# Layer 0's keys and values split straight into their attention tiles, with two tiles each, and the transposed maxima moved into the maxima's PSUM banks

## The chip, the cores and the metric

The kernel runs on one core of one Trainium2 chip. The time is the device time of one execution, in microseconds (us). The core has five engines that each work through a list of instructions of their own, strictly in order: TensorE (PE, matmuls; PEld is its weight load), VectorE (DVE), ScalarE (ACT), GpSimd (POOL) and SyncE (SP), which issues most DMA transfers. Engines wait for each other through semaphores.

## The reference

A two-layer model over 1024 latent tokens and 256 context tokens, width 1024. The change lies in layer 0, the even layer:

```python
aq, ak, av, ag, bq, bk, bv, bg = split_cols(h @ w_in, EVEN_WIDTHS)   # for latents and context
aq = rms_norm(heads(aq, A_HEADS), q_gain); ak = rms_norm(heads(ak, A_KV_HEADS), k_gain)
aq, ak, bq, bk = (apply_rope(t, cos, sin) for t in (aq, ak, bq, bk))  # latents only
oa = softmax(q k^T / 8) v     # branch A: every query block against all 1280 keys
ob = softmax(q k^T / 8 + band, sink) v   # branch B: context, and latents within +-128, with a sink logit
y = concat([oa * silu(ag), ob * silu(bg)]) @ w_out
```

Each branch has 8 query heads in 2 groups of 4 that share a key and value head. Layer 1 is a convolution module and a neighbourhood attention; its attention uses the same generator as layer 0's.

## The kernel before

All arithmetic is float32. A product is made from three matmuls of halves: each operand is split into a rounded high part (ACT copies it, L296) and the rest (`split`, L294 to 299, POOL or DVE subtracts). Layer 0 is cut into four **units**, one per key and value head: u = 2 and 3 are branch B, u = 0 and 1 branch A, in the order 2, 3, 0, 1 (`ORDER`).

- `proj_qkv(u)` (L772) projects 128 tokens at a time, ten blocks in five pairs, into PSUM (`pq`), copies them out (`pc`), norms and rotates them. `qk_tail` (L819) transposes a block (`trk`, in the one PSUM bank `tr`), splits queries and keys together (`qs`, 128x384) and stores them to DRAM (Q, K). Values are split into `vs` and stored to DRAM (V). `proj_gate` (L750, `pg`) makes the gates.
- Attention of a unit is ten groups of 128 queries x 4 heads (`group0`, L544). `attn_prep` (L378), two groups ahead, loads the queries (QH, QL), finds the maxima of the scores (`mx`, two PSUM banks, DVE reduces), and transposes them (`trn`, L404, in bank `tr`) into rows of QL. Then comes one **item** per 128 keys (L454): two matmuls to `st` (L463 against tile KA, L467 against tile KB), exp (L475), split into `ph` and `pl`, and `look` (3) items later three matmuls with the values (L426 to 428, `ov`). u = 2 and 3 have 42 items each, u = 0 and 1 have 84: 252 in all.
- KA (two buffers) holds the keys' high parts over their low parts; KB (one buffer) the high parts again and four rows of ones; V (one buffer) low and high values and a block of ones. All three are loaded from DRAM: KA in the prep of the unit's first group (`load_ka`, L535), KB at its first item (L540), V at its first `ov` (L629). The reload of KB and V must wait until the unit before has read them last. Earlier, the same SBUF holds modulation weights (`mw_tile`, L152).
- `weave` (L496) lays attention and **fill** side by side in the program: during a unit's attention the projections of the next one (`pq`, `pg`), during the last unit the output projection (`po`, L891). Fill has a lower priority, and a scheduler with a timeline of its own sets the final order on every engine, so a tile that it holds to be late draws fill forward.
- For the output projection `load_x1` (L883) loads the residual stream, 12 transfers on ACT's queue, between ACT's other work.

Of the kernel before, what the change touches and what calls it, by code (L numbers as in the profile page):

```python
# [87 lines left out]
def tile_kernel(ctx: ExitStack, tc: tile.TileContext, a, out):  # L88
# [22 lines left out]
    def nm(s):  # L111
        uid[0] += 1
        return f"{s}_{uid[0]}"
# [38 lines left out]
    def mw_tile():  # L152

        ring = MWR if mwp[0] is not None else "ABAV"
        mk[0] += 1
        t = ring[mk[0] % len(ring)]
        if t == "x":
            w = mwp[0].tile([P, 1024], F32, tag="mwx", name=nm("mw"), bufs=ring.count("x"))
        else:
            w = a0.tile([P, 1920 if t == "V" else NTOK], F32, tag={"A": "KA", "B": "KB", "V": "V"}[t], name=nm("mw"),  # L160
                        bufs=2 if t == "A" else 1)
        return w[:, 0:1024].rearrange("p (d n) -> p d n", d=2)
# [43 lines left out]
    def mod_steps(pool, halves):  # L206
# [10 lines left out]
        for n_, hf in enumerate(halves):  # L217
            for _ in range(4):
                yield
            tag = "ov" if solo[0] else "tr"  # L220
            pb = bank(tag, nm("pm"))
            for d, w in enumerate(ws):
                mod_part(pb, w, range(4 * d, 4 * d + 4))
            row = pool.tile([P, 512], F32, tag="macc", name=nm("mrow"), bufs=1)
            SC.copy(row, pb)
            yield
            yield
            mod_out(bank("ov" if solo[0] else "tr", nm("trm")), row, *hf)
# [149 lines left out]
    def attn_prep(pool, g):  # L378
# [22 lines left out]
        for _ in range(3):  # L401
            yield
        tr2 = bank("tr", nm("trn"))
        PE.transpose(tr2[0:nr, 0:P], nmt[:, 0:nr].bitcast(F32), ident)  # L404
# [111 lines left out]
    Qd = [[dram(f"Q{u}_{j}", [P, 2, 2, P]) for j in range(10)] for u in range(4)]  # L516
    Kd = [dram(f"K{u}", [64, 2, NTOK]) for u in range(4)]
    Vd = [dram(f"V{u}", [P, 10, P]) for u in range(4)]
    Gs = [dram(f"G{u}", [P, 2, NTOK]) for u in range(4)]
# [12 lines left out]

    KAs, KBs = [None] * 4, [None] * 4

    def load_ka(u):  # L535
        KAs[u] = a0.tile([P, NTOK], F32R, tag="KA", name=nm("KAt"), bufs=2)
        SY.dma_start(KAs[u][0:64, :].bitcast(F32), Kd[u][:, 0, :])
        SY.dma_start(KAs[u][64:128, :].bitcast(F32), Kd[u][:, 1, :])

    def load_kb(u):  # L540
        KB = KBs[0]
        SY.dma_start(KB[0:64, :].bitcast(F32), Kd[u][:, 0, :])

    def group0(u, qb):  # L544
        isb = u >= 2

        first = qb == QORD[0]

        def load_q(QH, QL):
            if first:  # L550
                load_ka(u)
            src = Qd[u][qb].rearrange("(e d) s a t -> d s e (a t)", e=2)
# [60 lines left out]
        def finish(ov, rb):  # L613
# [9 lines left out]
            else:  # L623
# [3 lines left out]

        hs = (u - 2) * 4
        g = Group(load_q=load_q, start=(lambda: load_kb(u)) if first else (lambda: None), bias=False, ahead=lambda t: None, gate=gate, v=lambda k: Vs[0][:, k, :], load_v=(lambda: SY.dma_start(Vs[0][:, :, 0:128].bitcast(F32), Vd[u])) if first else None, maxes=maxes, nmp=1 if qb < 2 else (2 if isb else 3),  # L629
                  sink=(sink[:, hs : hs + 4], sink8[:, hs : hs + 4]) if isb else None, skm=lambda: sk, k=lambda: (KAs[u], KBs[0]),  # L630
                  tiles=[(k, 0, 512, x) for k, x in kt], den=den, finish=finish)
# [6 lines left out]
    with ExitStack() as p0x:  # L638
# [133 lines left out]
        def proj_qkv(u, w):  # L772
            wh, wl = w or load_w0("ev_qkv", u)
            for jp in range(5):
                pc = ap.tile([P, 2, 384], F32, tag="pc", name=nm("pc"), bufs=PCB)
# [14 lines left out]
                if u < 2:  # L790
# [11 lines left out]
                SC.copy(vs[:, :, 1], pc[:, :, 320:384])  # L802
# [16 lines left out]
        def qk_tail(u, j, pc):  # L819

            tr = bank("tr", nm("trk"))
            for i in range(3):
                PE.transpose(tr[:, i * P : (i + 1) * P], pc[:, i * P : (i + 1) * P], ident)
# [726 lines left out]
```

## Time and profile before

| | |
|---|---|
| median of 3 runs | 1603.6 us (1599.02 to 1604.57) |
| the profiled execution, its own time | 1603.57 us |
| its span, first to last instruction | 1601.8 us |
| PE / DVE / POOL / ACT busy in the span | 92% / 67% / 49% / 46% |
| mean granted TensorE clock | 0.960 |
| bytes moved by DMA | 221.88 MB |

Layer 0's projections begin at 31 us, its attention at 149 us; its last item is at about 931 us. An engine's busy time is what its instructions took; since PE is near its limit, what counts is the time in which PE stood idle, and what it then waited for.

### The profile page before, as it was taken

To read this page: it belongs to the slowest core of one execution; us is meant where nothing else is said; L and a number is where in the kernel's file an instruction comes from. 1 tells how busy PE (TensorE), PEld (TensorE's weight loads), DVE (VectorE), ACT (ScalarE), POOL (GpSimd) and SP (SyncE) were. 2 spreads that over 40 slices of the span, in tenths; PEclk is the share of its full clock that TensorE was granted. 3 is DMA by queue.
4 is the path that set the end of the run, shared out by engine and by line. 5 is a ranking of instruction groups with operands and counts; after the bars stand their busy time and mean duration, and the time that the engine had idled before them with its cause. 6 is when DMAs were issued, how large, how long until landed. Compare 5 with 4: busy or idle time off the path is not lost.

```text
span 1601.8 us, 21782 instructions
## 1 busy us (share of the span) xinstructions
PE 1479.0 (92%) x7084; PEld 1181.1 (74%) x7084; DVE 1076.6 (67%) x2243; ACT 740.0 (46%) x1378; POOL 787.8 (49%) x632
## 2 busy tenths in 40 slices
PE   6899999998999989889999979999998899899995
PEld 2785978876788667668877757888877777777784
DVE  2921777497858677556488867999565476667776
ACT  4621343534344745644454754433343454545563
POOL 3530353554445755755554755654432343254575
PEclk9799999998999999989999989999999999999996
DMA  9476135342432123562111122213546777788732
GB/s 367 146 256 214 54 97 171 114 132 72 129 117 64 54 61 103 162 189 79 40 47 56 38 94 66 79 53 105 193 159 196 230 222 225 230 262 243 212 104 105
DMA packets 179194, 221.88 MB, mean 139 GB/s; under 512 B 16444, under 2 KB 120584, under 8 KB 179080
## 3 DMA queue, kind: packets, MB, share of 16 engines
q1 hardware_dynamic: 172416, 208.91, 42.2%
q10 hardware_dynamic: 6664, 11.57, 2.4%
q8 instruction: 56, 0.92, 0.2%
q14 instruction: 58, 0.48, 0.1%
HBM read 160.39 MB, written 60.03 MB: 138 GB/s over the span
## 4 chain that ended last, share of the span: by engine, by line
PE 66%; DVE 14%; DMA 8%; issue 6%; POOL 3%; ACT 2%; SPq 1%; DVEq 0%; ACTq 0%; POOLq 0%
PE p L317 5%; PE p L316 5%; PE p L318 5%; PE ov L426 4%; PE po L316 4%; PE ov L428 4%; PE ov L427 4%; PE po L317 4%; PE po L318 4%; PE st L463 3%; PE st L467 3%; PE pq L318 2%; PE pq L317 2%; PE pq L316 2%; PE pg L316 2%
## 5 line engine op out<-in xcount | busy, mean ns | idle before, releaser
L299 POOL TENSOR_TENSOR pl<-pf,ph 128x512 fp32r<-128x512 f32 (+4 forms) x321 | 391.7, 1233 | 341.2 <-ACT ph L296 294.8
L475 ACT ACTIVATE pf<-st 128x512 f32<-128x512 f32 x284 | 166.0, 597 | 212.7 <-PE st L467 158.4
L299 POOL TENSOR_TENSOR wl<-wr,wh 128x512 fp32r<-128x512 f32 (+2 forms) x131 | 169.4, 1306 | 172.0 <-ACT wh L296 146.5
L296 ACT CAST ph<-pf 128x512 fp32r<-128x512 f32 (+4 forms) x364 | 209.2, 588 | 32.3 <-PE ov L427 23.9
L316 PE MATMUL p<-hh,wh 128*128 128x512 f32 x448 | 181.3, 405 | 5.3 <-ACT hh L296 2.8
L317 PE MATMUL p<-hl,wh 128*128 128x512 f32 x448 | 180.0, 402 | 0.9 <-POOL hl L299 0.9
L318 PE MATMUL p<-hh,wl 128*128 128x512 f32 x448 | 177.7, 402 | 0.0
L463 PE MATMUL st<-QH,KAt 128*128 128x512 f32 (+4 forms) x364 | 142.9, 394 | 8.0 <-ACT pf L475 5.4
L426 PE MATMUL ov<-ph,Vt 128*128 128x512 f32 (+4 forms) x364 | 142.0, 390 | 5.8 <-DVE y L617 4.7
L428 PE MATMUL ov<-pl,Vt 128*128 128x512 f32 (+4 forms) x364 | 141.2, 388 | 3.9 <-DVE pl L299 2.5
L427 PE MATMUL ov<-ph,Vt 128*64 128x512 f32 (+4 forms) x364 | 139.8, 384 | 0.0
L467 PE MATMUL st<-QL,KBt 68*128 68x512 f32 (+4 forms) x364 | 137.7, 388 | 0.8 <-issue 0.8
L1035 DVE SCALAR_TENSOR_TENSOR cps<-U,taps,cps 128x512 f32<-128x512 f32 x184 | 126.3, 749 | 0.9
L296 ACT CAST wh<-wr 128x512 fp32r<-128x512 f32 (+2 forms) x134 | 80.7, 612 | 90.0 <-PE p L317 17.4
L580 DVE TENSOR_REDUCE mp<-mx 128x1 f32<-128x512 f32 x128 | 86.3, 683 | 53.4 <-PE mx L579 52.7
L316 PEld LDWEIGHTS p<-hh,wh 128*128 128x128 f32 x448 | 86.3, 193 | 27.3 <-ACT hh L296 3.0
L317 PEld LDWEIGHTS p<-hl,wh 128*128 128x128 f32 x448 | 85.9, 192 | 22.1 <-POOL hl L299 1.9
L318 PEld LDWEIGHTS p<-hh,wl 128*128 128x128 f32 x448 | 85.8, 191 | 20.0
L318 PE MATMUL pq<-wh,hl 128*128 128x384 f32 x256 | 89.4, 350 | 2.9 <-DVE hl L310 2.9
L316 PE MATMUL pq<-wh,hh 128*128 128x384 f32 x256 | 90.2, 352 | 0.8 <-ACT hh L296 0.7
L317 PE MATMUL pq<-wl,hh 128*128 128x384 f32 x256 | 89.3, 349 | 0.0
L428 PEld LDWEIGHTS ov<-pl,Vt 128*128 128x128 f32 x364 | 70.2, 193 | 25.8 <-POOL pl L299 3.8
(271 smaller groups left out, 3448.1 us busy)
## 6 DMA issues: line engine op xcount, KB each, us to landing
mw<-in_mod_w_dram SPq DMA_DIRECT2D x16, 1024.0 KB, 5.7
Q<-qs SPq DMA_DIRECT2D x40, 256.0 KB, 2.5
QH<-Q SPq DMA_DIRECT2D x80, 128.0 KB, 2.8
mw<-in_mod_w_dram SPq DMA_DIRECT2D x16, 512.0 KB, 7.2
wr<-in_od_d_dram SPq DMA_DIRECT2D x32, 256.0 KB, 2.8
wr<-in_ev_qkv_dram SPq DMA_DIRECT2D x16, 384.0 KB, 5.1
KAt<-KD SPq DMA_DIRECT2D x16, 384.0 KB, 6.5
wr<-in_od_wo_dram SPq DMA_DIRECT2D x22, 256.0 KB, 3.9
```

What stands on the lines that cost most here:

```text
L296: SC.copy(hi, src)
L299: (GP if leng == "g" else VE).tensor_tensor(lo, src, hi.bitcast(F32), op=ALU.subtract)
L316: PE.matmul(o, lh, rh, start=first, stop=False)
L317: PE.matmul(o, lh, rl, start=False, stop=False)
L318: PE.matmul(o, ll, rh, start=False, stop=last)
L426: PE.matmul(o, V[:, 64:192], ph[:, :n], start=(t == 0), stop=False)
L427: PE.matmul(g.ov[0:64, q0 : q0 + n], V[:, 0:64], ph[:, :n], start=False, stop=False)
L428: PE.matmul(o, V[:, 64:192], pl[:, :n], start=False, stop=(last and g.sink is None))
L463: sts.append(PE.matmul(st[:, :n], KA[:, cs], g.QH[:, q0 : q0 + n], start=True, stop=False))
L467: PE.matmul(st[:, :n], KB[0:68, cs], g.QL[0:68, q0 : q0 + n], start=False, stop=True)
L475: SC.activation(pf[:, :n], st[:, :n], AF.Exp, scale=1.0 if g.bias else SCALE)
L1035: VE.scalar_tensor_tensor(pc, uc, w, pc, op0=ALU.mult, op1=ALU.add)
```

## The change

Keys and values of layer 0 no longer pass through DRAM. `kv_tiles` allocates one KB, two KA and two V at the first projection (instead of at the start of the attention), and the units take turns on them. `qk_tail` splits the 64x128 of keys by two instructions of their own into KA, and the 128x256 of queries as before; `proj_qkv` writes the values' parts into V. KB is now loaded from KA, SBUF to SBUF, in two transfers (columns 0 to 511, then the rest), still at the unit's first item and still into one buffer. The transposed maxima (`trn`) take a bank of the maxima (`mx`) instead of `tr`, in both layers. Modulation weights may use two V buffers, and the row of a modulation product takes its memory from tag `rt2`.

```diff
@@ mw_tile
-                        bufs=2 if t == "A" else 1)
+                        bufs=1 if t == "B" else 2)
@@ mod_steps
-            row = pool.tile([P, 512], F32, tag="macc", name=nm("mrow"), bufs=1)
+            row = pool.tile([P, 640], F32, tag="rt2", name=nm("mrow"), bufs=2)[:, :512]
@@ attn_prep
-        tr2 = bank("tr", nm("trn"))
+        tr2 = bank("mx", nm("trn"))
@@ tile_kernel
-    def load_ka(u):
-        KAs[u] = a0.tile([P, NTOK], F32R, tag="KA", name=nm("KAt"), bufs=2)
-        SY.dma_start(KAs[u][0:64, :].bitcast(F32), Kd[u][:, 0, :])
-        SY.dma_start(KAs[u][64:128, :].bitcast(F32), Kd[u][:, 1, :])
+    KV = []
+    def kv_tiles():
+        KB = a0.tile([P, NTOK], F32R, tag="KB", name=nm("KBt"), bufs=1)
+        GP.memset(KB[64:68, :].bitcast(F32), 1.0)
+        for _ in range(2):
+            KA = a0.tile([P, NTOK], F32R, tag="KA", name=nm("KAt"), bufs=2)
+            V = a0.tile([P, 10, 192], F32R, tag="V", name=nm("Vt"), bufs=2)
+            GP.memset(V[:, :, 128:192].bitcast(F32), 1.0)
+            KV.append((KA, KB, V))
     def load_kb(u):
-        KB = KBs[0]
-        SY.dma_start(KB[0:64, :].bitcast(F32), Kd[u][:, 0, :])
+        for ks in (slice(0, 512), slice(512, NTOK)):
+            SY.dma_start(KBs[u][0:64, ks].bitcast(F32), KAs[u][0:64, ks].bitcast(F32))
+    def new_kv(u):
+        if not KV:
+            kv_tiles()
+        KAs[u], KBs[u], V0s[u] = KV[ORDER.index(u) % 2]
@@ group0
-            if first:
-                load_ka(u)
-    ... load_v=(lambda: SY.dma_start(Vs[0][:, :, 0:128].bitcast(F32), Vd[u])) if first else None
+    ... load_v=None
@@ proj_qkv
             wh, wl = w or load_w0("ev_qkv", u)
+            new_kv(u)
-                vs = ap.tile([P, 2, 2, 64], F32R, tag="vs", name=nm("vs"), bufs=2)
-                SC.copy(vs[:, :, 1], pc[:, :, 320:384])
-                GP.tensor_tensor(vs[:, :, 0], pc[:, :, 320:384], vs[:, :, 1].bitcast(F32), op=ALU.subtract)
-                SY.dma_start(Vd[u][:, 2 * jp : 2 * jp + 2], vs.rearrange("p j s d -> p j (s d)").bitcast(F32))
+                vs = V0s[u][:, 2 * jp : 2 * jp + 2, :]
+                SC.copy(vs[:, :, 64:128], pc[:, :, 320:384])
+                GP.tensor_tensor(vs[:, :, 0:64], pc[:, :, 320:384], vs[:, :, 64:128].bitcast(F32), op=ALU.subtract)
@@ qk_tail
-            qs = ap.tile([P, 2, 384], F32R, tag="qs", name=nm("qs"), bufs=2)
-            split(tr[:, 0:384], qs[:, 0, :], qs[:, 1, :], "s", "v")
-            SY.dma_start(Qd[u][j].rearrange("p a b t -> p a (b t)"), qs[:, :, 0:256].bitcast(F32))
-            mark[0] = SY.dma_start(Kd[u][:, :, j * P : (j + 1) * P], qs[0:64, :, 256:384].bitcast(F32))
+            qs = ap.tile([P, 2, 256], F32R, tag="qs", name=nm("qs"), bufs=2)
+            split(tr[:, 0:256], qs[:, 0, :], qs[:, 1, :], "s", "v")
+            mark[0] = SY.dma_start(Qd[u][j].rearrange("p a b t -> p a (b t)"), qs.bitcast(F32))
+            js = slice(j * P, (j + 1) * P)
+            split(tr[0:64, 256:384], KAs[u][0:64, js], KAs[u][64:128, js], "s", "v")
@@ before the attention
-        v_tiles(a0, 10)
-        KBs[0] = a0.tile([P, NTOK], F32R, tag="KB", name="KBt")
-        GP.memset(KBs[0][64:68, :].bitcast(F32), 1.0)
```

The order of instructions changes on every engine. Three places bear on what follows.

First, PE where the attention passes from u = 0 to u = 1. In the kernel before, the rows ahead of the first two reads of u = 1's KB (`st_7020`, `st_7053`); the last read of u = 0's KB stands 32 rows above the first of them:

```order
L463 MATMUL st_7053<-QH_6665,KAt_6667 128x512
L316 MATMUL po_7592<-hc_7273,wh_7578 128x256
L317 MATMUL po_7592<-hc_7273,wh_7578 128x256
L428 MATMUL ov_6913<-pl_6996,Vt_1149 128x512
L426 MATMUL ov_6913<-ph_7010,Vt_1149 128x512
L427 MATMUL ov_6913<-ph_7010,Vt_1149 64x512
L318 MATMUL po_7592<-hc_7273,wl_7585 128x256
L428 MATMUL ov_6913<-pl_7011,Vt_1149 128x512
L467 MATMUL st_7020<-QL_6666,KBt 128x512
L467 MATMUL st_7053<-QL_6666,KBt 128x512
```

and in the changed kernel from the last read of u = 0's KB (`st_6991`) to the first of u = 1's (`st_7005`):

```order
L467 MATMUL st_6991<-QL_6387,KBt_538 128x512
L587 MATMUL mx_6894<-KAt_543,QH_6832 128x512
L428 MATMUL ov_6897<-pl_6946,Vt_541 128x512
L426 MATMUL ov_6897<-ph_6963,Vt_541 128x512
L427 MATMUL ov_6897<-ph_6963,Vt_541 64x512
L463 MATMUL st_7005<-QH_6652,KAt_543 128x512
L467 MATMUL st_7005<-QL_6653,KBt_538 128x512
```

Of 31 rows, with output projection among them, five are left. At the two passages before this one it is the other way round: from the last read of a unit's KB to the next unit's first there were 37 and 65 rows, and now there are 88 and 83, fill for the most part.

Second, PE at u = 1's first maxima (the rows that read its KA). Before, they stand 27 rows behind the last transpose of u = 1's keys:

```order
L463 MATMUL st_6827<-QH_6314,KAt_4531 128x512
L467 MATMUL st_6827<-QL_6315,KBt 128x512
L567 MATMUL mx_6698<-KAt_6667,QH_6665 128x256 x2
L567 MATMUL mx_6717<-KAt_6667,QH_6665 128x256 x2
L428 MATMUL ov_6733<-pl_6782,Vt_1149 128x512
```

and in the changed kernel 703 rows behind it, each group's first maxima right behind a `trn`:

```order
L463 MATMUL st_6796<-QH_6297,KAt_540 128x512
L467 MATMUL st_6796<-QL_6298,KBt_538 128x512
L404 MATMUL trn_6628<-ident,nmt_6610 4x128
L575 MATMUL mx_6682<-KAt_543,QH_6652 128x256 x2
L428 MATMUL ov_6717<-pl_6746,Vt_541 128x512
```

The keys' transposes have moved far forward, with the rest of u = 1's projection.

Third, DVE in the start-up, where the normed inputs are made (`xr_344` and `xr_336` are the first 512 latents, `xr_59` to `xr_66` the second; `hl` are low parts that the projection needs). Before:

```order
L306 SCALAR_TENSOR_TENSOR xr_65_381<-xr_65_381,gs_95,bc_496 128x512
L306 SCALAR_TENSOR_TENSOR xr_66_382<-xr_66_382,gs_95,bc_496 128x512
L310 SCALAR_TENSOR_TENSOR hl_173<-xr_344,modT_93,hh_172 128x512 x4
L310 SCALAR_TENSOR_TENSOR hl_175<-xr_62_378,modT_93,hh_174 128x512
L310 SCALAR_TENSOR_TENSOR hl_175<-xr_63_379,modT_93,hh_174 128x512
```

and in the changed kernel:

```order
L306 SCALAR_TENSOR_TENSOR xr_336<-xr_336,gs_95,bc_419 128x512 x8
L241 SCALAR_TENSOR_TENSOR nr_482<-nt_483,nr_482 128x4
L310 SCALAR_TENSOR_TENSOR hl_165<-xr_336,modT_93,hh_164 128x512 x4
L306 SCALAR_TENSOR_TENSOR xr_59_367<-xr_59_367,gs_95,bc_488 128x512
L306 SCALAR_TENSOR_TENSOR xr_60_368<-xr_60_368,gs_95,bc_488 128x512
```

The first half's low parts now stand ahead of the second half's products, not behind them.

More of the change, by code (lines that the diff above doesn't have):

```diff
@@ L516, in tile_kernel @@
     Qd = [[dram(f"Q{u}_{j}", [P, 2, 2, P]) for j in range(10)] for u in range(4)]
-    Kd = [dram(f"K{u}", [64, 2, NTOK]) for u in range(4)]
-    Vd = [dram(f"V{u}", [P, 10, P]) for u in range(4)]
     Gs = [dram(f"G{u}", [P, 2, NTOK]) for u in range(4)]
@@ L531, in tile_kernel @@
     VE.tensor_scalar(sink8, sink, 8.0, None, op0=ALU.mult)
-    KAs, KBs = [None] * 4, [None] * 4
-    def load_ka(u):
-        KAs[u] = a0.tile([P, NTOK], F32R, tag="KA", name=nm("KAt"), bufs=2)
-        SY.dma_start(KAs[u][0:64, :].bitcast(F32), Kd[u][:, 0, :])
-        SY.dma_start(KAs[u][64:128, :].bitcast(F32), Kd[u][:, 1, :])
-    def load_kb(u):
-        KB = KBs[0]
-        SY.dma_start(KB[0:64, :].bitcast(F32), Kd[u][:, 0, :])
+    KAs, KBs, V0s = [None] * 4, [None] * 4, [None] * 4
+    KV = []
[7 more added lines that the diff above has]
+            KV.append((KA, KB, V))
+    def load_kb(u):
+        for ks in (slice(0, 512), slice(512, NTOK)):
[4 more added lines that the diff above has]
+        KAs[u], KBs[u], V0s[u] = KV[ORDER.index(u) % 2]
     def group0(u, qb):
         isb = u >= 2
-        first = qb == QORD[0]
         def load_q(QH, QL):
-            if first:
-                load_ka(u)
             src = Qd[u][qb].rearrange("(e d) s a t -> d s e (a t)", e=2)
@@ L628, in group0 @@
         hs = (u - 2) * 4
-        g = Group(load_q=load_q, start=(lambda: load_kb(u)) if first else (lambda: None), bias=False, ahead=lambda t: None, gate=gate, v=lambda k: Vs[0][:, k, :], load_v=(lambda: SY.dma_start(Vs[0][:, :, 0:128].bitcast(F32), Vd[u])) if first else None, maxes=maxes, nmp=1 if qb < 2 else (2 if isb else 3),
-                  sink=(sink[:, hs : hs + 4], sink8[:, hs : hs + 4]) if isb else None, skm=lambda: sk, k=lambda: (KAs[u], KBs[0]),
+        g = Group(load_q=load_q, start=(lambda: load_kb(u)) if qb == QORD[0] else (lambda: None), bias=False, ahead=lambda t: None, gate=gate, v=lambda k: V0s[u][:, k, :], load_v=None, maxes=maxes, nmp=1 if qb < 2 else (2 if isb else 3),
+                  sink=(sink[:, hs : hs + 4], sink8[:, hs : hs + 4]) if isb else None, skm=lambda: sk, k=lambda: (KAs[u], KBs[u]),
                   tiles=[(k, 0, 512, x) for k, x in kt], den=den, finish=finish)
```

## Prediction

> **What bounds the kernel now.** I read the page first, then the stretches of the span, the waits of PE, and the timeline at its longest wait. On the page:
>
> ```profile
> span 1601.8 us, 21782 instructions
> PE 1479.0 (92%) x7084; PEld 1181.1 (74%) x7084; DVE 1076.6 (67%) x2243; ACT 740.0 (46%) x1378; POOL 787.8 (49%) x632
> ```
>
> PE is the bound. The change adds and removes no matmul, so all that it can win or lose is PE's idle time (1601.8 - 1479.0 = 122.8 us) and time at a low clock. By stretches (columns: length, then busy time and count of PE, PEld, DVE, ACT, POOL, granted PE clock, DMA share, GB/s):
>
> ```profile
> 0.00:160.00 160.00, 138.77 (x690) 96.87 (x690) 65.76 (x131) 58.96 (x113) 49.72 (x45) 0.95 0.72 246
> 160.00:320.00 160.00, 157.42 (x831) 135.66 (x830) 105.54 (x279) 68.47 (x141) 70.31 (x56) 0.99 0.36 109
> 320.00:480.00 160.00, 149.30 (x749) 121.94 (x749) 122.05 (x328) 65.76 (x130) 76.56 (x58) 0.96 0.38 113
> 480.00:720.00 240.00, 215.30 (x972) 166.55 (x972) 158.67 (x317) 130.01 (x226) 148.87 (x112) 0.95 0.35 105
> 720.00:920.00 200.00, 196.69 (x950) 157.59 (x949) 141.99 (x252) 107.84 (x197) 115.38 (x91) 1.00 0.18 53
> 920.00:1601.00 681.00, 621.55 (x2901) 502.50 (x2899) 482.55 (x939) 308.96 (x574) 326.93 (x274) 0.95 0.54 163
> ```
>
> Layer 0's attention has 2.6 + 10.7 + 24.7 + 3.3 = 41.3 us of idle PE, most of it from 480 to 720 us. The waits of PE there (line, releaser: total, times, longest):
>
> ```profile
> PE mx L567 <- DMA KAt<-K: 8.2, 1, 8.2
> PE pg L316 <- ACT pc L785: 4.7, 3, 2.3
> PE trk L823 <- DVE QL L405: 3.1, 2, 2.8
> ```
>
> The first is the load of u = 1's KA. No row names the loads of KB or V as a wait of PE, so the second V buffer by itself frees nothing. The rest of the idle time is short waits where attention has no fill beside it:
>
> ```profile
> 520.00:560.00 40.00, 36.05 (x154) 25.08 (x153) 24.97 (x51) 30.10 (x51) 29.12 (x24) 1.00 0.18 52
> 520.00:560.00 40.00, 9.51 (x24) 1.00 0.18 52
> 480.00:720.00 240.00, 35.39 (x89) 0.95 0.35 105
> 720.00:920.00 200.00, 29.81 (x77) 1.00 0.18 53
> ```
>
> The last three count L467 alone, one per item: 24 items without fill cost 3.95 us of idle, 0.165 us each. From 720 to 920 us, where the output projection lies between them, 77 items cost 3.31 us, 0.043 each.
>
> **The change, term by term.** All against the profiled execution, 1603.57 us (1.8 us outside its span), equal to the median of 1603.6.
>
> *A, the wait for KA.* In the timeline:
>
> ```profile
> 677.72 0.48 ACTq L887 DMA_DIRECT2D x<-in_cT_dram  x1
> 677.97 0.59 SPq L538 DMA_DIRECT2D KAt<-K  x1
> 685.33 0.38 ACTq L887 DMA_DIRECT2D x<-in_xT_dram  x1
> 685.81 0.60 ACT L475 ACTIVATE pf<-st 128x512 f32<-128x512 f32 x1 [6.95 <-DMA KAt<-K]
> 687.36 1.19 PE L567 MATMUL mx<-KAt,QH 128*128 128x256 f32 x4 [8.16 <-DMA KAt<-K]
> 688.35 0.63 PE L428 MATMUL ov<-pl,Vt 128*128 128x512 f32 x1
> 692.61 0.50 PE L579 MATMUL mx<-KAt,QH 128*128 128x512 f32 x1
> 693.87 0.39 PE L463 MATMUL st<-QH,KAt 128*128 128x512 f32 x1
> 694.10 0.40 PE L467 MATMUL st<-QL,KBt 68*128 68x512 f32 x1
> ```
>
> PE idles 8.16 us. The ten matmuls behind it start 0.43 us apart (4.26 us from 688.35 to 692.61) instead of 0.23, so the clock was low: 4.26 - 2.35 = 1.9 us more. The load and its store are gone, and u = 1's keys are now split 703 rows ahead: 10.1 us. But ACT stood still at the same time, between two issues of the residual's loads (L887, 677.72 and 685.33), and these twelve loads stay. They now meet u = 0's attention, and PE has some 2.5 us of matmuls before it needs ACT. If ACT is held as long, 4.5 us stay; the 640 KB of KA are gone from its neighbourhood, so I take 4. A = -6.1; bounds -10.1 (all hidden) and -3 (all 7 us shown).
>
> *B, where the fill lies.* Counted in the changed order, items 141 to 160 have 36 matmuls of fill, 161 to 180 have 7, 201 to 220 have 18; before, the poor part was 101 to 120 (none), later ones having about 100 in twenty. So of items 81 to 252, 60 are poor: 60 x 0.165 + 112 x 0.043 = 14.7 us, against 24.7 + 3.3 - 8.2 = 19.8 before: -5.1. Bounds: 0 (the poor part as dear as 480 to 720 was) and -10 (look-ahead hides it). The clock belongs to it:
>
> ```profile
> 560.00:600.00 40.00, 35.01 (x151) 26.17 (x150) 30.18 (x61) 19.87 (x36) 22.66 (x18) 0.91 0.19 57
> ```
>
> The clock was below 1 there, 0.955 over 520 to 600 us. Before, 480 to 720 lost 0.05 x 240 = 12 us, 10.1 without A's; after, 60 poor items of 40 / 24 = 1.67 us are 100 us, 4.5 us lost. Half of the difference, since part of a low clock falls on idle time: -2.8. The Trainium skill (TensorE: Matmul & The Clock Gate, What's actually happening) lets the clock drop only after an idle window of about 3.4 us. By that rule the short waits here would cost no clock and this -2.8 would be 0; the row, with no wait of PE in it above the 2.3 us listed, speaks for a loss, and I follow the row.
>
> *C, KB of u = 1.* From the last old read to the first new one only five rows are left, 5 x 0.23 = 1.2 us, and no fill. Nearest rows of the first 128 KB, and the removed transfers:
>
> ```profile
> QL<-Q SPq DMA_DIRECT2D x40, 128.0 KB, 2.8
> KBt<-K SPq DMA_DIRECT2D x4, 320.0 KB, 4.0
> Vt<-V SPq DMA_DIRECT2D x4, 640.0 KB, 4.7
> K<-qs SPq DMA_DIRECT2D x40, 64.0 KB, 2.1
> V<-vs SPq DMA_DIRECT2D x20, 128.0 KB, 2.2
> ```
>
> 2.8 - 1.2 = 1.6, 4.0 - 1.2 = 2.8: C = +2.0; no gain is possible, since nothing was lost there. The second part is read four items later, some 6 us. The Trainium skill (SBUF — State Buffer, The DMA setup-cost knee) asks for one large transfer, since each pays about 2 us whatever its size; its fit gives an estimate of 2.3 us for 128 KB, by which C would be +1.1. SP loses 76 of these transfers and gains 8; none was waited for but KA.
>
> *D, units 2 and 3.* The wait of `trk` for QL (3.1) goes, since `trn` leaves bank `tr`. Against it stand instructions:
>
> ```profile
> L299 DVE TENSOR_TENSOR qs<-trk,qs 128x384 fp32r<-128x384 f32 x40 | 22.1, 552 | 41.6 <-ACT qs L296 37.5 <-DMA wr<-in_ev_g_dram 4.0
> L617 DVE TENSOR_TENSOR y<-ov,rb 64x256 f32<-64x256 f32 x80 | 33.1, 413 | 1.1
> L296 ACT CAST qs<-trk 128x384 fp32r<-128x384 f32 x40 | 19.2, 479 | 41.5 <-PE trk L823 41.5
> L802 ACT CAST vs<-pc 128x128 fp32r<-128x128 f32 x20 | 6.1, 303 | 0.2
> 320.00:360.00 40.00, 38.05 (x194) 30.11 (x194) 37.29 (x105) 15.03 (x30) 20.38 (x17) 0.98 0.44 131
> ```
>
> On DVE, 139 ns for 128 elements more make a 128-wide subtraction 274 ns; 413 + 274 - 552 = 135 ns, 40 times: 5.4 us. DVE is full where u = 0's projection meets u = 3's attention (37.29 of 40 us), so I count half, 2.7. On ACT, 391 + 303 - 479 = 215 ns, 40 times: 8.6 us, hidden beside PE at 46% busy; shown in full it would be +8.6. D = -0.4; bounds -3.1 and +5. The 64x640 of ones for the second V cost POOL about 0.6 us in the start-up, hidden.
>
> *E, the start-up.*
>
> ```profile
> 53.66 10.62 DVE L306 SCALAR_TENSOR_TENSOR xr<-xr,gs,bc 128x512 f32<-128x512 f32 x16
> 64.20 9.88 DVE L310 SCALAR_TENSOR_TENSOR hl<-xr,modT,hh 128x512 fp32r<-128x512 f32 x8
> 65.36 0.69 PE L318 MATMUL pq<-wh,hl 128*128 128x384 f32 x1 [2.56 <-DVE hl L310]
> ```
>
> PE waits 2.56 us for the first `hl` of DVE, which comes behind sixteen products; now it comes behind eight, 8 x 0.66 = 5.3 us earlier. E = -2.6; bounds -4 (with the low clock behind it) and 0 (the second half's inputs then late).
>
> *F, `trn` among the maxima,* 56 times in both layers: it holds one of two banks until DVE has made QL.
>
> ```profile
> DVE QL L405 <- PE trn L404: 28.8, 15, 4.0
> ```
>
> DVE waits for PE there, so the bank is freed soon: +1.0; the other end is the second rival's.
>
> Sum: -6.1 - 5.1 - 2.8 + 2.0 - 0.4 - 2.6 + 1.0 = -14.0. 1603.6 - 14.0 = 1589.6 us.
>
> **The rivals.** *The gain is eaten* (0.26): the poor items cost what 480 to 720 cost, and ACT's hold shows in full. For it: ACT was held 6.95 us by loads that stay. Against: fill is drawn forward, so items 20 to 140 are richer than before. A -3, B 0, C +2.8, D -0.4, E -2.6, F +1: 1601.4.
>
> *Slower* (0.10): the ring of the maxima binds. Behind each `trn` the next group's second maxima must wait until DVE, in its own order, has made QL; if that is 0.5 us late on average, 56 x 0.5 = 28 us, and with the other terms (-15.0) 1603.6 + 13.0 = 1616.6. It decides from 15.0 / 56 = 0.27 us each. For it: `trk` did wait up to 2.8 us for QL. Against: the row above, and that PE has other rows between.
>
> *More* (0.13): ACT's hold falls where PE has fill, the look-ahead hides the poor items. A -10.1, B -10, C +1.6, D -3.1, E -4, F 0: 1578.
>
> **How the numbers follow.** Forecast 0.51. About 0.5%, 8 us, can be told from no change. Of the forecast's 0.51 some 0.46 lie below 1595.6; with 0.13 that makes faster 0.59. The remaining 0.05 and the first rival make same 0.31, slower is 0.10. The range takes in the first rival with the bounds around it and most of the third: 1579 to 1608.
>
> **What would show it.** In the changed profile PE's waits should name neither KA nor QL ahead of `trk`; PE should idle some 13 to 22 us from item 81 to 252, most of it between items 141 and 180 and at u = 1's first L467 (about 2 us); L306 and L310 should alternate at 59 us, with no PE wait at 65. A wait of PE on ACT at the residual's loads longer than 5 us would make A too large; PE waits at L575 on QL would make F wrong; a layer 1 longer by more than 3 us would too.

## The result, and the profile after

Six runs of the changed kernel have a median of 1592.7 us (1589.1 to 1595.1), six of the kernel before beside them 1604.1 us. The ratio is 0.9929, its 95% interval 0.9909 to 0.9950: faster by 0.7%. The forecast was 1589.6 us. The total came out near it; most of its terms did not, as the following sections show.

The profiled execution took 1590.1 us (before 1603.6). Its page:

```profile
span 1588.3 us, 21721 instructions
PE 1477.4 (93%) x7084; PEld 1178.0 (74%) x7084; DVE 1087.8 (68%) x2283; ACT 745.3 (47%) x1418; POOL 791.0 (50%) x633
```

PE has the same 7084 matmuls and is as long busy. Its idle time fell from 122.8 to 110.9 us, by 11.9 of the 13.5 us that the spans differ (the medians differ by 11.4). Three of the stretches shown of before:

```profile
0.00:160.00 160.00, 138.49 (x705) 97.09 (x706) 71.57 (x168) 64.42 (x134) 53.77 (x50) 0.91 0.63 221
...
480.00:720.00 240.00, 231.67 (x1084) 180.73 (x1084) 161.40 (x322) 126.72 (x233) 147.33 (x111) 0.99 0.32 102
720.00:920.00 200.00, 180.94 (x795) 134.59 (x795) 155.42 (x282) 125.57 (x228) 127.40 (x101) 0.96 0.14 42
```

From 480 to 720 us PE's idle time fell from 24.7 to 8.3 us, and from 720 to 920 us it rose from 3.3 to 19.1. What the first stretch won, the second gave back. The waits of PE that answer to those shown of before:

```profile
PE st L463 <- ACT pf L475: 8.1, 7, 3.1
...
PE ov L426 <- DVE y L625: 6.2, 5, 2.3
...
PE trk L831 <- DVE KAt L299: 3.7, 1, 3.7
...
PE pq L316 <- ACT hh L296: 2.8, 1, 2.8
...
PE mx L575 <- DVE QL L405: 2.0, 3, 1.1
...
PE mx L575 <- DMA QH<-Q: 1.6, 1, 1.6
...
PE mx L1267 <- DVE QL L405: 0.7, 2, 0.4
```

The wait for KA (8.2) is gone, and no load of KB or V stands in its place. `trk` waits for DVE's new split of the keys instead of for QL, and the start-up's wait for `hl` (2.9) has become one of 2.8 us for ACT's `hh`.

Equal times hold different work, so the fair cuts are by the work itself: the first L467, u = 0's first, u = 1's first, layer 0's last, layer 1's first projection (`p`), the end. Before:

```profile
0.00:173.85 173.85, 152.62 (x768) 110.14 (x769) 71.32 (x150) 61.49 (x119) 50.18 (x46) 0.95 0.68 233
173.85:505.46 331.61, 318.15 (x1628) 266.42 (x1628) 244.50 (x637) 140.77 (x281) 159.82 (x122) 0.97 0.37 110
505.46:724.41 218.95, 194.43 (x868) 148.20 (x868) 139.38 (x274) 121.66 (x210) 136.84 (x102) 0.95 0.36 108
724.41:930.56 206.15, 201.07 (x961) 159.75 (x960) 144.14 (x257) 115.76 (x212) 123.60 (x97) 1.00 0.16 47
930.56:957.79 27.23, 18.06 (x64) 13.04 (x63) 18.57 (x33) 13.84 (x29) 13.96 (x14) 0.75 0.35 114
957.79:1601.80 644.01, 594.70 (x2801) 483.57 (x2799) 458.65 (x894) 286.49 (x529) 303.37 (x253) 0.96 0.55 168
```

and the changed kernel:

```profile
0.00:152.90 152.90, 131.39 (x666) 92.38 (x666) 66.72 (x151) 58.40 (x122) 49.91 (x46) 0.91 0.65 228
152.90:517.93 365.03, 349.80 (x1821) 294.83 (x1820) 270.70 (x704) 153.61 (x327) 168.12 (x129) 0.98 0.31 98
517.93:733.91 215.98, 210.64 (x980) 164.64 (x979) 138.24 (x255) 117.58 (x208) 137.88 (x103) 0.98 0.31 100
733.91:927.17 193.26, 174.75 (x765) 130.60 (x763) 144.82 (x262) 120.42 (x220) 121.71 (x98) 0.95 0.14 41
927.17:948.92 21.75, 17.34 (x60) 12.44 (x59) 12.02 (x19) 8.35 (x16) 10.36 (x8) 0.84 0.42 136
948.92:1588.30 639.38, 593.52 (x2800) 483.09 (x2800) 455.29 (x894) 286.99 (x529) 303.04 (x253) 0.96 0.56 169
```

The counts of PE's matmuls show how fill moved: 102 fewer in the start-up, 193 more beside units 2 and 3, 112 more beside u = 0, 196 fewer beside u = 1, where less of it was left. Length less busy time is PE's idle time. Start-up: 21.2 before, 21.5 now; units 2 and 3: 13.5, 15.2; u = 0: 24.5, 5.3; u = 1: 5.1, 18.5; from there to `p`: 9.2, 4.4; the rest: 49.3, 45.9. In the attention of u = 0 and 1 together, on which the prediction rested, 5.8 us were won; 4.8 behind it and 3.4 in layer 1, on which it counted nothing; the start-up and units 2 and 3 gave back 2.0. These are single executions; the table below shows how far they can be read.

### The profile page after: what moved, and what is told of

Read it like the earlier page. It is cut to its first block, busy times and chain, and to the rows that moved or that the text cites. A ratio compares the mean times of both kernels' runs of the same rounds, so it can differ in the third digit from the quotient of the medians.

```text
span 1588.3 us, 21721 instructions
## 1 busy us (share of the span) xinstructions
PE 1477.4 (93%) x7084; PEld 1178.0 (74%) x7084; DVE 1087.8 (68%) x2283; ACT 745.3 (47%) x1418; POOL 791.0 (50%) x633
## 4 chain that ended last, share of the span: by engine, by line
PE 67%; DVE 16%; DMA 7%; issue 4%; ACT 2%; POOL 2%; SPq 0%; DVEq 0%; ACTq 0%; POOLq 0%
PE p L316 6%; PE p L317 6%; PE p L318 6%; PE ov L426 4%; PE ov L428 4%; PE ov L427 4%; PE st L463 4%; PE st L467 3%; PE po L316 3%; PE po L317 3%; PE po L318 3%; PE pq L316 3%; PE pq L317 3%; PE pq L318 3%; PE pg L318 2%
## 5 line engine op out<-in xcount | busy, mean ns | idle before, releaser
L467 PE MATMUL st<-QL,KBt 68*128 68x512 f32 (+4 forms) x364 | 136.6, 388 | 0.0
L463 PEld LDWEIGHTS st<-QH,KAt 128*128 128x128 f32 x364 | 70.1, 193 | 28.1 <-ACT pf L475 12.1
L426 PEld LDWEIGHTS ov<-ph,Vt 128*128 128x128 f32 x364 | 70.5, 194 | 23.9 <-issue 6.9
```

Source lines behind the costliest of these rows:

```text
L426: PE.matmul(o, V[:, 64:192], ph[:, :n], start=(t == 0), stop=False)
L463: sts.append(PE.matmul(st[:, :n], KA[:, cs], g.QH[:, q0 : q0 + n], start=True, stop=False))
L467: PE.matmul(st[:, :n], KB[0:68, cs], g.QL[0:68, q0 : q0 + n], start=False, stop=True)
```

## The experiments

Each kernel was timed against the kernel before on the same chip. The idle time of PE in each profiled execution, by the same cuts (us), with the ratio of the times:

| Kernel | start | units 2, 3 | u = 0 | u = 1 | to `p` | rest | ratio (95%) |
|---|---|---|---|---|---|---|---|
| before | 21.2 | 13.5 | 24.5 | 5.1 | 9.2 | 49.3 | 1 |
| changed | 21.5 | 15.2 | 5.3 | 18.5 | 4.4 | 45.9 | 0.9929 (0.9909, 0.9950) |
| trn back in `tr` | 21.0 | 20.6 | 13.7 | 3.2 | 5.4 | 44.4 | 0.9908 (0.9885, 0.9930) |
| trn back, layer 0 only | 21.2 | 23.0 | 14.3 | 5.1 | 5.7 | 48.4 | 0.9909 (0.9886, 0.9932) |
| trn alone | 23.0 | 20.6 | 12.0 | 20.4 | 3.5 | 51.2 | 1.0058 (1.0036, 1.0080) |
| tails early | 23.2 | 16.0 | 26.7 | 5.1 | 9.0 | 51.3 | 0.9981 (0.9961, 1.0000) |
| fill held, 20 | 21.1 | 27.4 | 19.6 | 8.9 | 8.7 | 47.4 | 1.0079 (1.0061, 1.0098) |
| fill held, 40 | 20.5 | 26.3 | 11.5 | 14.3 | 3.9 | 43.7 | 0.9977 (0.9959, 0.9994) |
| trn mixed | 22.7 | 18.0 | 18.4 | 4.9 | 10.0 | 47.5 | 0.9954 (0.9939, 0.9970) |
| KB in one | 22.8 | 15.4 | 7.1 | 19.5 | 4.0 | 48.3 | 0.9949 (0.9928, 0.9969) |
| V through DRAM, one tile | 23.3 | 20.9 | 6.2 | 18.1 | 6.1 | 47.3 | 1.0030 (1.0015, 1.0045) |
| V through DRAM, two tiles | 22.6 | 16.7 | 12.0 | 19.7 | 4.7 | 47.3 | 0.9944 (0.9925, 0.9962) |
| rotation on POOL | 22.9 | 20.6 | 6.4 | 18.6 | 4.7 | 48.6 | 0.9980 (0.9960, 1.0000) |
| the same, trn back | 23.3 | 22.8 | 12.4 | 3.8 | 8.6 | 48.7 | 0.9892 (0.9872, 0.9911) |

How much two executions differ can be read from pairs of kernels. 'Changed' and 'KB in one' have the same order of PE's rows in the start-up, in units 2 and 3, from layer 0's last item to `p` and in the rest; the first two kernels with trn back have the same order up to `p`. Within these pairs an entry differs by up to 2.4 us, so a difference of 3 us or less between two entries shows nothing.

The theories after the result were two: 'place' (what counts is where fill lies, and trn's move drew it forward) and 'ends' (the gain lies behind the two attentions and comes from trn's move).

**trn put back**, in both layers or in layer 0 alone:

```diff
-        tr2 = bank("mx", nm("trn"))
+        tr2 = bank("tr", nm("trn"))                   # trn back
+        tr2 = bank(("tr", "mx")[layer[0]], nm("trn")) # layer 1 only
```

> The changed kernel with trn put back into bank tr; keys and values still go straight into the double-buffered tiles. In its order the fill stands as it stood before (items 160 to 252 have about 100 matmuls of it in each twenty; the changed kernel has 7 to 119). Theory 'place': trn's move drew the fill forward and so cost in 720 to 920 us what it won before; the direct keys are worth the KA wait and its slow clock by themselves. Then the wait of mx for KA is gone, 480 to 720 us has 12 to 16 us of idle PE, 720 to 920 us 3 to 6, item 252 starts near 920 us, and the time is 1587 to 1595 us. Theory 'ends': of the 13.5 us that the two profiles differ, 9.3 lie behind the two attentions (from item 252 to layer 1's first p, and behind layer 1's last item), and they come from trn having left bank tr. Then they come back: item 252 near 926 us, 28 us from there to the first p, 40 us behind layer 1's last item, 1599 to 1603 us.

> As the kernel with trn back in bank tr, but in layer 1 trn stays in the ring of the maxima. Theory 'place': layer 0 as with trn back (item 252 near 920 us), and the stretch behind layer 1's last item is 37 us instead of 40 if trn made that, else the same: 1584 to 1595 us. Theory 'ends': layer 1's end is won alone, 3 to 4 us less than with trn back in both layers, 1595 to 1600 us.

Medians 1592.5 and 1591.6 us (0.9908, 0.9909). So trn's bank in layer 1 makes no difference that can be told, and 'ends' falls: both times are below the 1595 to 1603 us that it gave, and without trn's move the stretch to `p` still has 5.4 us of idle time. With trn back, units 2 and 3, u = 0 and u = 1:

```profile
156.48:491.41 334.93, 314.29 (x1567) 263.23 (x1567) 224.69 (x610) 142.78 (x295) 151.71 (x116) 0.93 0.31 100
491.41:713.90 222.49, 208.77 (x981) 166.51 (x981) 160.10 (x327) 124.72 (x229) 143.03 (x107) 0.98 0.32 99
713.90:925.39 211.49, 208.30 (x987) 167.30 (x986) 143.95 (x257) 118.81 (x214) 126.74 (x99) 0.98 0.15 46
```

Beside u = 0 and 1 PE idles 16.9 us, the changed kernel 23.8, the kernel before 29.6; units 2 and 3 pay for it (20.6 us, clock 0.93). At u = 1's first maxima (671.2 us) PE no longer waits, but at those of its second group it does:

```profile
PE mx L575 <- DMA QH<-Q: 3.8, 1, 3.8
```

This Q was issued at 680.1 and 680.7 us, among the twelve loads of the residual (679.0 to 693.0), and landed at 689.2, where the median of such a load is 2.7 us. Behind the wait the clock fell for some 3.4 us (matmuls of 512 columns 0.43 us apart from 690.6). With trn back in layer 0 alone, where PE has the same order, the same wait is 2.1 us and the clock stays full.

**trn moved, nothing else:**

```diff
-        tr2 = bank("tr", nm("trn"))
+        tr2 = bank("mx", nm("trn"))
```

> The kernel before with nothing changed but trn in the ring of the maxima. Its order draws the fill further forward than the changed kernel does: none of it in items 120 to 140, 12 and 18 matmuls in the next two twenties. Theory 'place': a wait for u = 1's KA stays, the poor items now reach it, and 720 to 920 us idles 15 to 20 us: 1602 to 1612 us. Theory 'ends': the two ends are won without anything else, 9 us: 1593 to 1597 us.

1615.1 us, 0.6% slower than before. That is the direction that 'place' gave, 3 us above its range, and 720 to 920 us idles 18.1 us as it said. But one of its reasons is wrong: PE has no wait for KA at all. The projection ran so far ahead that the old way through DRAM was in time. Either half of the change removes that wait, so their gains can't be added. What trn's move costs stands among its waits and in u = 1's row:

```profile
PE trn L404 <- DVE nmt L394: 10.2, 7, 5.9
...
PE trn L404 <- DVE nmt L400: 7.2, 3, 5.8
```

```profile
756.76:949.59 192.83, 172.42 (x747) 129.16 (x748) 137.41 (x248) 120.36 (x219) 119.48 (x96) 0.94 0.13 42
```

PE waits 17.4 us for the maxima that trn transposes (8.3 in the changed kernel, 3.1 before), and idles 20.4 us beside u = 1.

**Tails early**, the kernel before:

```diff
-                for _ in range(2):
-                    if tails:
-                        qk_tail(*tails.pop(0))
+                while tails:
+                    qk_tail(*tails.pop(0))
```

> The kernel before, with all waiting tails of a unit's projection done at the first block of its gate instead of two at each block, so that u = 1's keys are stored in DRAM some 40 us earlier; fill and banks as before. It tries term A by itself. If the load of KA was the wait: mx on KA is gone or below 2 us, and the time is 8 to 10 us lower, 1593 to 1597 us. If the twelve loads of the residual held ACT whatever KA did: PE waits 4 to 7 us for ACT at those loads, and the time is 1598 to 1602 us. If the tails only crowd DVE earlier: no difference to before.

1603.8 us: no difference that can be told. The edit missed its aim: u = 1's last keys were still stored at 679.6 us, KA still issued at 682.1, and PE waited 8.3 us. It says nothing on term A.

**Fill held to its place, and trn mixed** (the first with 20, later 40, items):

```diff
-                weave(main, n1, fill0(k + 1), NFILL[k], False)
+                weave(main, n1, fill0(k + 1), NFILL[k], False, lag=20)
...
```

```diff
-        tr2 = bank("mx", nm("trn"))
+        tr2 = bank("mx" if layer[0] or g.sink is not None else "tr", nm("trn"))
```

> The changed kernel, in which each step of layer 0's fill may start only behind the L463 that stands 20 items back in the program, so that fill can't run far ahead. In its order items 80 to 160 then have 102, 114, 24 and 96 matmuls of fill in each twenty, 160 to 252 103, 132, 159, 120 and 90 (the changed kernel 174, 89, 193, 36 and 7, 119, 18, 84, 48). Theory 'place': items without fill cost, and fill that is drawn forward is missing later. Then 720 to 920 us has 4 to 8 us of idle PE instead of 19.1, 480 to 720 us 8 to 14, and the time is 1574 to 1586 us. Rival 'conserved': the fill is a fixed amount, and wherever it is taken from PE idles as long: 1588 to 1596 us.

> The changed kernel with trn in the ring of the maxima for units 2 and 3 and layer 1, in bank tr for units 0 and 1. In its order the fill stands as in the changed kernel up to item 80, has none in items 80 to 120, and from 140 on stands as in the kernel before. Theory 'place': items 40 to 84 cost what they cost in the changed kernel (with trn back in tr, 320 to 480 us idled 20.6 us at a clock of 0.86, in the changed kernel 8.9 us at 0.97), 720 to 920 us idles 3 to 6 us, the 40 items without fill cost 5 to 8 us more: 1580 to 1589 us. Rival 'conserved': 1588 to 1596 us.

> As the kernel with its fill held, but 40 items back instead of 20. In its order the fill of items 0 to 60 is that of the changed kernel, 60 to 80 has 143 matmuls of it instead of 185 (72 and 48 when held at 20), and from 80 on the twenties have 114, 24, 83, 116, 122, 135, 95, 73 and 48 (changed: 174, 89, 193, 36, 7, 119, 18, 84, 48). Theory 'pace': in units 2 and 3 DVE sets the pace, so fill costs nothing there and what is held back from there is paid for later: item 40 to 84 took 187.1 us before, 173.4 in the changed kernel and 181.2 when held at 20, with 144 matmuls of fill less than in the changed kernel. Then this kernel takes 173 to 178 us there, item 168 comes within 3 us of the changed kernel's 732.5 less the work put off, 720 to 920 us idles 8 to 14 us instead of 19.1, and the time is 1580 to 1588 us. Rival 'scatter': where small waits come together the clock drops whatever the fill is, and evening it out gains nothing: 1590 to 1602 us.

1615.0, 1595.1 and 1600.9 us. All are above the ranges of 'place' and 'pace', which so fall as they were put. Of the rivals, 'conserved' gave the time of trn mixed but not that of fill held at 20, which is above both its ranges; 'scatter' gave the time of fill held at 40. (A count was off by one in the expectations: u = 0's first item of the changed kernel starts at 517.9 us, so item 40 to 84 took it 192.3 us, not 173.4.) Holding fill did what was meant beside u = 1 (8.9 us idle, changed 18.5), and lost more elsewhere. Held at 20, units 2 and 3, and u = 1:

```profile
152.66:506.62 353.96, 326.57 (x1646) 272.09 (x1644) 251.91 (x641) 142.49 (x301) 153.75 (x118) 0.95 0.30 96
...
714.87:945.03 230.16, 221.23 (x1051) 176.05 (x1049) 149.97 (x270) 123.48 (x219) 131.74 (x104) 0.99 0.20 64
```

Against the changed kernel's rows: in units 2 and 3, 175 matmuls fewer save only 11.1 us, and beside u = 0, 115 fewer (208.25 us, 865) save 7.7, while beside u = 1, 286 more cost 36.9 us. What was held back was paid for at twice what it saved. The matmuls that moved are not of one width, so this is the price of this move and not of fill as such; that an even spread would be best, as 'place' had it, is refuted. Held at 40, units 2 and 3 took longer than in the changed kernel with fewer matmuls (370.5 us, 1759), so the price is no constant either.

**KB in one transfer:**

```diff
-        for ks in (slice(0, 512), slice(512, NTOK)):
-            SY.dma_start(KBs[u][0:64, ks].bitcast(F32), KAs[u][0:64, ks].bitcast(F32))
+        SY.dma_start(KBs[u][0:64, :].bitcast(F32), KAs[u][0:64, :].bitcast(F32))
```

> The changed kernel with KB loaded in one transfer instead of two (first 512 keys, then the rest). In the changed kernel the first part for u = 1 was issued at 722.6 us and the second at 733.4 us, and PE did not wait. Theory: the split itself hides the load, since the first 512 keys are last read six items before the others; one transfer must wait for all of them, and PE waits 1.5 to 3 us at the first L467 of units 3, 0 and 1: 2 to 7 us longer than the changed kernel, 1594 to 1600 us. Rival: PE's order has enough other rows there, products with V and maxima, so the load is hidden either way: within 2 us of the changed kernel.

1596.4 us; its ratio can't be told from the changed kernel's. The place shows the mechanism: the transfer was issued at 732.9 us, and PE's first read of it waited:

```profile
736.77 0.70 PE L467 MATMUL st<-QL,KBt 68*128 68x512 f32 x2 [0.86 <-DMA KBt<-KAt]
```

0.9 us, below the 1.5 that was expected, and no wait for KB at units 3 and 0: other rows of PE cover the rest.

**V through DRAM** again, with one tile and with two (keys direct, trn moved):

```diff
-                vs = V0s[u][:, 2 * jp : 2 * jp + 2, :]
...
+                vs = ap.tile([P, 2, 2, 64], F32R, tag="vs", name=nm("vs"), bufs=2)
...
+                SY.dma_start(Vd[u][:, 2 * jp : 2 * jp + 2], vs.rearrange("p j s d -> p j (s d)").bitcast(F32))
```

> The changed kernel with V as before: through DRAM, one V tile, loaded at each unit's first product; the keys go straight into their tiles. Theory: the second V tile frees nothing, since no wait of PE named a load of V: 1588 to 1597 us, and no wait of PE for V above 1 us. Rival: V's load comes behind the old unit's last product and PE waits 2 us or more at the first ov of units 3, 0 and 1: 1597 to 1603 us.

> As the kernel with V through DRAM, but with two V tiles in turn instead of one (the staging tile vs has one buffer instead of two, for room). It splits what V's part of the change brought, 0.3% above the kernel before with one tile and 0.7% below it with the changed kernel's direct tiles. If the second tile made it (the load no longer waits for the old unit's last product): 1590 to 1597 us. If the route through DRAM made it (stores and loads on SP and the DMA queues): 1604 to 1610 us. If neither, but the order that came out of it: anywhere, with the difference in items 40 to 84, where the kernel with one tile lost 11 us.

1608.0 and 1596.4 us. The second V tile is worth 0.9% (0.9944 against 1.0030), and the route through DRAM nothing that can be told from the direct tiles (0.9944, 0.9929). Two things beside the tile differ between these kernels: with one V tile the modulation weights have one V buffer too, and with two the staging tile `vs` has one buffer instead of two. Neither was tried alone, so the 0.9% belong to the tile together with them. The theory behind the first of the two falls, and its rival too, whose range ended at 1603 us. Yet with one tile PE hardly waits for V; among what the rows that use the V tile waited for stands (us, times):

```profile
  DMA Vt<-V: 0.3, 1
```

So it is not a load that is late; that the tile works through the order of the rows, which is another, is likely but not shown. Where it does is not settled: the two profiled executions differ by 4.5 us only (1606.6 and 1602.1 us, the second the slowest of its nine runs), and their idle times by stretch differ both ways.

**The rotation's product on POOL**, in the changed kernel and with trn back:

```diff
-                    VE.tensor_tensor(p5, p5, kcs[:, 0, 2 * jp - 2 : 2 * jp, None, :].broadcast_to([P, 2, 5, 64]),
+                    GP.tensor_tensor(p5, p5, kcs[:, 0, 2 * jp - 2 : 2 * jp, None, :].broadcast_to([P, 2, 5, 64]),
```

> The changed kernel with one product of the rotation of queries and keys (L821, 128x640, 990 ns on DVE, once per token pair of a projection) moved from DVE to POOL. Fill stands as in the changed kernel to within some ten matmuls. It tries whether DVE sets the pace of units 2 and 3: between 160 and 500 us ten such products are 9.9 us of DVE. Theory 'pace': item 40 to 84 (173.4 us in the changed kernel) takes 3 to 8 us less, total 1583 to 1590 us. Rival: DVE is busy there but does not set the end, since PE idled only 8.9 us from 320 to 480 us in the changed kernel; then nothing is gained, 1590 to 1596 us, or POOL's slower product makes the tails late, 1594 to 1600 us.

> The same product moved to POOL in the kernel with trn back in bank tr. That kernel lost most between items 40 and 84: 320 to 480 us had 20.6 us of idle PE at a clock of 0.86, with DVE busy 38.41 of the 40 us from 360 to 400. Theory 'pace': with DVE relieved by 9.9 us in this part, that idle time falls to 8 to 14 us and the clock there rises above 0.92, 1578 to 1587 us in all. Rival: the waits of trk for QL and KA in bank tr are a matter of order, not of DVE's load; then 1589 to 1596 us.

1601.4 us, slower than the changed kernel (item 40 to 84 took 206.3 us, there 192.3; the product took 1563 ns on POOL, 990 on DVE); and 1587.2 us, the lowest of all, though it can't be told from the kernel with trn back alone (0.9908), and its interval just touches the changed kernel's. 'Pace' falls with the first. In the second, PE idles 22.8 us from 320 to 480 us (20.6 with trn back alone, 8 to 14 expected) at a clock of 0.90, though DVE was 7 us less busy in units 2 and 3 (217.7 us, 224.7). So DVE's load alone does not set it:

```profile
320.00:480.00 160.00, 137.18 (x658) 108.62 (x657) 119.09 (x331) 67.42 (x139) 83.52 (x62) 0.90 0.29 93
...
943.73:1586.50 642.77, 594.09 (x2801) 482.73 (x2800) 455.89 (x894) 286.53 (x529) 305.01 (x253) 0.96 0.55 169
```

The last row matters for layer 1. On PE this kernel's layer 1 stands row for row as in the kernel before, and there its 48.7 us of idle time are those of before (49.3), with the same wait for Q of 9.1 us:

```profile
PE mx L1259 <- DMA QH<-QD: 9.1, 4, 3.8
```

In the changed kernel the order of layer 1 is another, though nothing in layer 1 but trn's bank was edited, and that wait is 0.8 us. The run with KB in one transfer has the changed kernel's order in layer 1 row for row, and there that wait is 0.9 us:

```profile
948.48:1586.10 637.62, 589.35 (x2801) 478.53 (x2800) 455.83 (x894) 287.16 (x529) 303.27 (x253) 0.97 0.56 170
```

Yet it idles 48.3 us, as long as before within 1.0. So the wait for Q went with the order, but the 3.4 us of idle time that the changed kernel's layer 1 seemed to win are not shown to come from it.

## Why the prediction came out right, step by step

The sum was right, its terms were not: what fill did was mis-sized, and gains from places that had not been looked at made up for it.

*A, the wait for KA* (-6.1). It went: at u = 1's first maxima (715.6 us) PE waits for nothing. The residual's loads are now issued from 580.0 to 591.8 us, beside u = 0. ACT's hold behind them did come (ACT stood 4.1 us up to 592.3, with issues of these loads at 587.2 and 590.5), but PE did not wait for it. What PE lost there is a wait of 1.6 us for the Q of u = 0's fifth group, at 580.6 us, and clock:

```profile
576.00:600.00 24.00, 21.82 (x90) 16.24 (x89) 15.97 (x29) 13.85 (x24) 17.76 (x13) 0.86 0.97 343
```

24 us at 0.86 lose 3.4. If both are put down to the loads, which no run shows, A is 8.2 + 1.9 - 1.6 - 3.4 = 5.1 us won, else up to 10.1. With the fill in its old place (trn back) 3.8 us of waiting and 1.7 of clock stay, and A is -4.6; with trn back in layer 0 alone 2.1 us stay, and it is -8.0. The size was sound. The means was not: PE waited for a transfer of Q and not for ACT, and lost clock. And the direct keys are not the only thing that removes the wait for KA: with trn alone it is gone too.

*B, where the fill lies* (-5.1, clock -2.8). This is the step that failed. Beside u = 0 and 1 PE idles 23.8 us where the forecast's poor and rich items made 14.7. Taken from before to after, the idle time there fell by 5.8 us; 8.2 - 1.6 = 6.6 of that lies at KA's wait and what replaced it, so B brought +0.8, nothing that can be told from 0, where -5.1 was forecast. The price by item was the error. In the changed kernel items 141 to 180, 181 to 200, 201 to 220 and 221 to 252:

```profile
687.60:757.10 69.50, 66.82 (x290) 48.67 (x289) 48.14 (x85) 49.73 (x84) 52.42 (x40) 1.00 0.19 55
757.10:813.80 56.70, 53.28 (x250) 42.32 (x249) 39.55 (x77) 27.31 (x47) 27.05 (x21) 0.97 0.14 38
813.80:850.10 36.30, 34.94 (x145) 25.73 (x145) 27.64 (x50) 25.63 (x45) 24.41 (x19) 0.96 0.14 45
850.10:927.20 77.10, 64.63 (x279) 46.59 (x278) 62.37 (x112) 51.92 (x102) 53.54 (x45) 0.91 0.09 31
```

and items 221 to 252 before:

```profile
856.90:930.60 73.70, 69.13 (x329) 52.89 (x327) 61.58 (x110) 49.96 (x93) 50.29 (x41) 1.00 0.11 40
```

The 60 items that were called poor, 141 to 180 and 201 to 220, idle 2.7 and 1.4 us, 4.0 in all: 0.07 us each, less than half of the 0.165 that they were given. The dear ones are the last 32, which were priced at 0.043 us each and idle 12.5 us, 0.39 each, where before they idled 4.6. Twenty of them have fill beside them (72 matmuls, 84 before). So whether fill lies beside an item does not give its price. PE waits there for ACT's `pf` (5.8 us) and for DVE's `y` (3.3) and `x` (1.9); why these are late is open. One thing seen and not tried: from 850 to 905 us DVE does 16.5 us of work on the norm of layer 0's output (L306, L310, L939), and in the same twenty items before 4.9 (L306, L933). The forecast counted fill by its matmuls alone.

The sum for B was also not of like with like. It set a price for after against the measured 19.8 us of before; by the same prices before makes 20 x 0.165 + 152 x 0.043 = 9.8 us, and B would have been a loss of 4.9.

Of the clock's -2.8 nothing shows. Busy time times the missing clock was 194.4 x 0.05 = 9.7 us beside u = 0 and 1 before, 210.6 x 0.02 + 174.8 x 0.05 = 13.0 after: 3.3 more. But the first two kernels with trn back, in one and the same order, differ by as much (208.8 x 0.02 + 208.3 x 0.02 = 8.3 us, and 207.9 x 0.02 = 4.2), so even the sign can't be told. That short waits do cost clock, the trace shows:

```profile
809.34 0.47 PE L426 MATMUL ov<-ph,Vt 128*128 128x512 f32 x1 [2.33 <-DVE y L625]
...
810.41 0.63 PE L427 MATMUL ov<-ph,Vt 128*64 128x512 f32 x1
810.84 0.63 PE L428 MATMUL ov<-pl,Vt 128*128 128x512 f32 x1
...
816.10 0.63 PE L467 MATMUL st<-QL,KBt 68*128 68x512 f32 x1
816.52 0.63 PE L463 MATMUL st<-QH,KAt 128*128 128x512 f32 x1
```

From 810 to 817 us matmuls start 0.43 us apart, behind a wait of 2.3 us. The Trainium skill (TensorE: Matmul & The Clock Gate, What's actually happening) has the clock fall after an idle window of about 3.4 us; no wait of PE from 790 to 885 us is longer than 3.14. So the row was rightly followed against the rule.

*C, KB of u = 1* (+2.0). It cost nothing. SP issued its two parts here:

```profile
722.59 0.50 SPq L548 DMA_DIRECT2D KBt<-KAt  x1
...
733.39 0.56 SPq L548 DMA_DIRECT2D KBt<-KAt  x1
```

and PE's last read of the old KB and first of the new:

```profile
732.52 0.39 PE L467 MATMUL st<-QL,KBt 68*128 68x512 f32 x1
...
733.68 0.40 PE L463 MATMUL st<-QH,KAt 128*128 128x512 f32 x1
733.91 0.40 PE L467 MATMUL st<-QL,KBt 68*128 68x512 f32 x1
```

The five rows between are right, and the wrong ones to count: the first part holds keys 0 to 511, whose last read is six items earlier. It was issued 11.3 us ahead of the first read. Even in one transfer the price was 0.9 us. The Trainium skill (SBUF — State Buffer, The DMA setup-cost knee) asks for one large transfer, and its fit gave an estimate of 2.3 us for the first part; the parts landed in 2.2 to 3.2 us, and here the split saved PE the 0.9 us, since each part could leave as soon as its readers were done; in the whole time that can't be told.

*D, units 2 and 3* (-0.4). `trk` no longer waits for QL, 3.7 us for KA's split came instead. The instructions cost what was estimated on DVE and less on ACT:

```profile
L299 DVE TENSOR_TENSOR qs<-trk,qs 128x256 fp32r<-128x256 f32 x40 | 16.8, 419 | 36.9 <-ACT qs L296 36.7
L296 ACT CAST qs<-trk 128x256 fp32r<-128x256 f32 x40 | 14.9, 373 | 23.3 <-PE trk L831 14.7 <-issue 7.1 <-DMA gt<-G 1.4
L299 DVE TENSOR_TENSOR KAt<-trk,KAt 64x128 fp32r<-64x128 f32 x40 | 11.4, 284 | 8.1 <-ACT KAt L296 7.4
L296 ACT CAST KAt<-trk 64x128 fp32r<-64x128 f32 x40 | 10.4, 259 | 37.2 <-DVE qs L299 37.2
```

419 + 284 - 552 = 151 ns (135 estimated) and 373 + 259 - 479 = 153 ns (215). Idle time in units 2 and 3 rose by 1.7 us, with a clock of 0.98 instead of 0.97; neither can be told from nothing. With trn back the same instructions stand beside 20.6 and 23.0 us of idle time and clocks of 0.93 and 0.95, beyond the bound of +5; there less fill lies beside them too, so trn's leaving bank `tr` is one difference and not the only one.

*E, the start-up* (-2.6). PE's idle time did not fall (21.2, 21.5): `hl` came early, and the next thing late was ACT's `hh`, 2.8 us. The forecast had moved one wait and not asked what stood behind it. The clock of the start-up was lower as well, 0.91 instead of 0.95 (0.93 with KB in one, in the same order).

*F, trn among the maxima* (+1.0). PE waited 2.0 + 0.7 us for QL at the maxima, small, as forecast. But trn's move did something else: the whole fill ran ahead (1926 matmuls in units 2 and 3 with trn alone, 1628 before). The likely reason is that the projections' transposes no longer had to take turns with the groups' `trn` in one bank; that was not tried apart. Alone this makes the kernel 0.6% slower; with direct keys and two V tiles 0.2%, not to be told from nothing. The rival that priced it (each maxima late by 0.5 us) had the sign, not the mechanism.

*The second V buffer* was said to free nothing by itself, since no row named a load of V, and stood in the sum with nothing. With the two buffers that changed beside it, it is worth 0.9%, and so it is the largest gain among the parts: trn alone 1.0058, with direct keys 1.0030, with the second V tile 0.9944, with direct values 0.9929.

*What was not in the sum.* Behind layer 0's attention 4.8 us of idle time went; the six other kernels with the changed kernel's order there idle 3.5 to 6.1 us too. In layer 1 3.4 us went in this execution, of which the run with the same order there shows 1.0. That these made up for B is luck: nothing in the prediction foresaw them.

What stays open: why units 2 and 3 idle between 13.5 and 27.4 us in these kernels. Neither the amount of fill nor DVE's load alone explains it. Also open is by what way the second V tile gains.

## What to carry to other kernels

Where a scheduler orders the work, moving a small tile to another bank can change the order of the whole program; take the fill's new place from the order first, count what it brings to every engine and not its matmuls alone, and price the kernel before and after in the same way. A buffer that no wait names can still be worth something. And a total that comes out right is no proof of its terms: cut both traces at the same pieces of work, compare term by term, and read from two executions of the same order how much of a difference is noise.

## What was not expected of the hardware

The clock fell behind a wait of 2.3 us: matmuls of 512 columns then started 0.43 instead of 0.23 us apart for some 7 us. But the length of the wait alone does not decide it here: with trn back in layer 0 alone the clock stayed full behind one of 2.1 us, and in the changed kernel it was 0.86 over the 24 us around one of 1.6.
